# First products from transposed x with the norm's factor put on results, and another order in the scan, the prelude and the projections

## The chip, the cores and the metric

One core of a Trainium2 chip runs the whole layer in one launch. The metric is the device time of the run in microseconds; lower is better. Three runs of the kernel before were timed, and one more was profiled.

## The reference

x is 512 tokens by 2048 channels in float32. The layer is, cut to what matters:

```python
h = rmsnorm(x, norm_w)                  # x * rsqrt(mean(x*x) + eps) * w, per token
u = h @ w_in
z_ssm, xbc, dt_f, dt_b, q_a, kv_a, z_attn, g_ssm, g_attn = split(u)
xs, bm, cm = split(silu(dwconv(xbc, conv_w, conv_b)))        # conv over 4 tokens
y = ssd_scan(xs, dtf, a_f, bm, cm) + flip(ssd_scan(flip(xs), flip(dtb), a_b, flip(bm), flip(cm))) + d_skip * xs
y = rmsnorm_by_group(y * silu(z_ssm), ssm_norm_w)            # 4 groups of 512 channels
q  = rmsnorm(q_a, q_norm_w) @ w_uq                           # 16 heads, 128 + 64 (rotary)
kv = rmsnorm(kv_a[:512], kv_norm_w) @ w_ukv
o = softmax_attention(q, kv, rotary key) * silu(z_attn)
merged = sigmoid(g_ssm) * (y @ w_proj_ssm) + sigmoid(g_attn) * (o @ w_proj_attn)
out = rmsnorm(x + merged @ w_out, final_norm_w)
```

The factor rsqrt(mean(x*x) + eps) is one number per token. Since it is the same for all channels of a token, (x * w * factor) @ W equals ((x * w) @ W) * factor.

## The kernel before

**Products.** A float32 operand is split into a high part (ACT casts it to the reduced format, `wh`, L163 or L432) and a low part (DVE subtracts, `wl`, L164 or L433), and each product is three matmuls, high by high, high by low and low by high (`mm3`, L167 to L170; in the Strassen products L562 to L564). One matmul has a 128x128 stationary operand and 512 columns; a tile of 128 output channels takes 16 steps of three. Weights come in chunks of 128x1024 (512 KB) through three raw buffers (`wraw`) and three buffers for each part. `wchunk` (L157) issues load, cast and subtraction of a chunk with a priority offset `ahead[0]`, which is AHEAD (60) nearly everywhere.

**Order.** PE runs in the order in which the code issues its matmuls. The other engines' orders come from a scheduler that sorts by place in the program, moved ahead by the offset of `tc.high_priority`.

**Stages.** (1) x is loaded token by token rows, ACT squares it with a running sum (L210), a short DVE chain makes the factor, DVE scales x (L220), PE transposes it in 64 blocks (L225) and ACT and DVE split the result, times `norm_w`, into `h_h` and `h_l` (L229, L230). (2) Seven tiles: dt (`dtp`) and the six xbc tiles of scan group 0; after each, convolution and SiLU. Between them `h_sums` adds `h_h` and `h_l` back together and makes the sums of blocks of h that Strassen's scheme needs (S1, S2, S4). `dt_make` makes dt and writes it to the scratch `dt_d`. (3) Three gate projections (wz, wgs, wga), each as two column pairs of seven Strassen products (P1 to P7, `Strassen.pair`). A product is four chunks of 12 matmuls. Sums of weight blocks are made while they are loaded, by accumulating DMA (`w_more`), or by DVE. A headed pair takes P1 and P2 beforehand (`Strassen.head`, with P1b and P2b for the second pair); here only the ssm projection (`wps`) does that. (4) Four groups of the scan (`ssd_group`). Group 0 first transposes dt (`dt_turn`, L308) and sums it (`dt_sums`, L317 to L320). Every group loads B, C and four x tiles from scratch, transposes them (L872, `post_b`, `post_x`), makes local states ("loc", from `xw_h` and `xw_l`, L931 and L932) and adds up the diagonal parts ("yb", L1016). `y_norm` then gates and scales a y tile and `y_turn` transposes it (L848). Between these steps `gap()` runs fill work, the next group's xbc tiles and the qkv and za tiles, in shares listed in `shares`:

```python
shares = [0.7] * 2 + [0.8] * 6 + [1.25] * 10
left = [0, (10 * 48, 10 * 48, 9 * 48, 10 * 48)[g] / sum(shares)]
```

The first share stands ahead of the transpositions, the second ahead of "loc". After the last group the rest of za runs beside the normalising of the compressed q and kv (`compressed`, L1072 and L1074). (5) Sixteen attention heads, with their own fill; `r_sum` (L326) sums squares over channels for the q and kv norms with one matmul ("rp", L328) into the bank `pc`, which the diagonal sums use too. (6) The two branch projections and the output projection; the head of `wps` is fill of the last two attention heads, and what remains of it is issued by `fill.all()` after the loads and splits of S1 and S2 (operand sums read from scratch `yn_d`).

## Time and profile before

| | us |
|---|---|
| three timed runs | 2066.1, 2069.7, 2075.88 (median 2069.7) |
| the profiled execution, its own time | 2068.9 |
| its span | 2066.8 |
| PE busy in it | 1970.5 (95%) |
| DVE busy | 1463.1 (71%) |
| ACT busy | 959.3 (46%) |
| DMA, mean | 183 GB/s |

The span runs from the first to the last instruction of the profiled execution. Busy time is the union of an engine's instructions. PEld is the loading of stationary operands, which overlaps the matmuls. In a timeline a row has the start, the length, engine, line, operation and tiles, and in brackets how long the engine stood idle before it and what released it.

### The profile page before, as it was taken

To read this page: it belongs to the slowest core of one execution; us is meant where nothing else is said; L and a number is where in the kernel's file an instruction comes from. 1 tells how busy PE (TensorE), PEld (TensorE's weight loads), DVE (VectorE), ACT (ScalarE), POOL (GpSimd) and SP (SyncE) were. 2 spreads that over 40 slices of the span, in tenths; PEclk is the share of its full clock that TensorE was granted. 3 is DMA by queue.
4 is the path that set the end of the run, shared out by engine and by line. 5 is a ranking of instruction groups with operands and counts; after the bars stand their busy time and mean duration, and the time that the engine had idled before them with its cause. 6 is when DMAs were issued, how large, how long until landed. Compare 5 with 4: busy or idle time off the path is not lost.

```text
span 2066.8 us, 24703 instructions
## 1 busy us (share of the span) xinstructions
PE 1970.5 (95%) x9074; PEld 1627.3 (79%) x9074; DVE 1463.1 (71%) x1946; ACT 959.3 (46%) x1344; POOL 315.9 (15%) x337
## 2 busy tenths in 40 slices
PE   6999999999989999899899999999998999999998
PEld 5888888888867877787788788788877787888886
DVE  7976676676659689788786666667576888776342
ACT  6444444444444545445555344444444444443232
POOL 0011010010042151332420001110010111100110
PEclk9999999999999999999999999999999999999999
DMA  5567657656556837677564857873376876865332
GB/s 195 168 173 197 182 121 187 194 124 171 144 171 186 243 120 191 225 211 219 166 182 150 240 166 185 217 199 96 85 213 251 294 245 250 268 227 168 104 120 82
DMA packets 166584, 378.56 MB, mean 183 GB/s; under 512 B 16000, under 2 KB 65280, under 8 KB 165888
## 3 DMA queue, kind: packets, MB, share of 16 engines
q1 hardware_dynamic: 104688, 238.33, 35.2%
q0 software_dynamic: 26944, 92.29, 20.5%
q10 hardware_dynamic: 34832, 46.38, 6.3%
q8 instruction: 71, 1.16, 0.2%
q14 instruction: 49, 0.40, 0.1%
HBM read 325.03 MB, written 98.04 MB: 205 GB/s over the span
## 4 chain that ended last, share of the span: by engine, by line
PE 69%; DVE 11%; DMA 9%; issue 6%; ACT 2%; POOL 1%; SPq 0%; ACTq 0%; DVEq 0%; POOLq 0%
PE P L563 10%; PE P L564 10%; PE P L562 10%; PE f L1485 3%; PE f L1486 3%; PE f L1484 3%; PE za L168 2%; PE za L169 2%; PE za L170 2%; PE xbc L168 2%; PE xbc L169 2%; PE xbc L170 2%; DVE wl L164 2%; DVE sum L995 1%; DMA wraw<-wps 1%
## 5 line engine op out<-in xcount | busy, mean ns | idle before, releaser
L433 DVE TENSOR_TENSOR wl<-X,wh 128x1024 fp32r<-128x1024 f32 x152 | 185.2, 1222 | 81.8 <-ACT wh L432 81.3
L432 ACT CAST wh<-X 128x1024 fp32r<-128x1024 f32 x152 | 159.6, 1053 | 160.0 <-PE P L564 134.6
L164 DVE TENSOR_TENSOR wl<-wraw,wh 128x1024 fp32r<-128x1024 f32 (+2 forms) x148 | 175.4, 1186 | 81.7 <-ACT wh L163 76.4
L163 ACT CAST wh<-wraw 128x1024 fp32r<-128x1024 f32 (+2 forms) x150 | 145.3, 969 | 157.4 <-PE xbc L169 43.5
L433 DVE TENSOR_TENSOR wl<-wraw,wh 128x1024 fp32r<-128x1024 f32 x74 | 91.3, 1233 | 98.5 <-ACT wh L432 98.3
L168 PE MATMUL xbc<-h_h,wh 128*128 128x512 f32 x384 | 151.8, 395 | 0.0
L170 PE MATMUL xbc<-h_h,wl 128*128 128x512 f32 x384 | 150.2, 391 | 0.1
L169 PE MATMUL xbc<-h_l,wh 128*128 128x512 f32 x384 | 150.0, 391 | 0.0
L433 DVE TENSOR_TENSOR wl<-Y,wh 128x1024 fp32r<-128x1024 f32 x80 | 97.8, 1223 | 73.1 <-ACT wh L432 73.0
L563 PE MATMUL P<-wl,h_h 128*128 128x512 f32 x384 | 149.4, 389 | 0.0
L564 PE MATMUL P<-wh,h_l 128*128 128x512 f32 x384 | 149.4, 389 | 0.0
L562 PE MATMUL P<-wh,h_h 128*128 128x512 f32 x384 | 149.4, 389 | 0.0
L432 ACT CAST wh<-wraw 128x1024 fp32r<-128x1024 f32 x74 | 78.0, 1054 | 146.0 <-PE f L1486 71.0
L432 ACT CAST wh<-Y 128x1024 fp32r<-128x1024 f32 x80 | 84.2, 1053 | 114.8 <-PE P L564 95.3
L563 PE MATMUL P<-wl,S 128*128 128x512 f32 x288 | 112.4, 390 | 0.6 <-DVE wl L433 0.6
L564 PE MATMUL P<-wh,S 128*128 128x512 f32 x288 | 112.1, 389 | 0.0
L562 PE MATMUL P<-wh,S 128*128 128x512 f32 x288 | 112.1, 389 | 0.0
L170 PE MATMUL za<-h_h,wl 128*128 128x512 f32 x256 | 101.2, 395 | 5.0 <-DVE wl L164 5.0
L168 PE MATMUL za<-h_h,wh 128*128 128x512 f32 x256 | 102.3, 400 | 0.0
L169 PE MATMUL za<-h_l,wh 128*128 128x512 f32 x256 | 100.6, 393 | 0.0
L170 PEld LDWEIGHTS xbc<-h_h,wl 128*128 128x128 f32 x384 | 72.3, 188 | 16.1 <-DVE small L841 0.6
L168 PEld LDWEIGHTS xbc<-h_h,wh 128*128 128x128 f32 x384 | 72.6, 189 | 15.0 <-issue 0.2
(634 smaller groups left out, 5189.0 us busy)
## 6 DMA issues: line engine op xcount, KB each, us to landing
wraw<-wi SPq DMA_DIRECT2D x102, 512.0 KB, 4.1
da<-da_d SPq DMA_DIRECT2D x64, 256.0 KB, 4.4
T_wps<-wps POOLq DMA_DIRECT2D x32, 512.0 KB, 6.2
T_wpa<-wpa POOLq DMA_DIRECT2D x32, 512.0 KB, 9.9
wraw<-wo SPq DMA_DIRECT2D x32, 512.0 KB, 3.4
wraw<-wps SPq DMA_DIRECT2D x24, 512.0 KB, 5.0
xbc_d<-xbc ACTq DMA_DIRECT2D x24, 256.0 KB, 2.9
wraw<-wun SPq DMA_DIRECT2D x16, 384.0 KB, 3.1
```

The lines of the kernel that those rows point to most:

```text
L163: act.copy(h, raw)
L164: (dve if ahead[0] else pool).tensor_sub(l, raw, h.bitcast(F32))
L168: pe.matmul(out, wh, xh, start=start, stop=False)
L169: pe.matmul(out, wh, xl, start=False, stop=False)
L170: pe.matmul(out, wl, xh, start=False, stop=stop)
L432: act.copy(hi_, raw)
L433: dve.tensor_sub(lo_, raw, hi_.bitcast(F32))
L562: pe.matmul(bs[i], xh, wh, start=(j == 0), stop=False)
L563: pe.matmul(bs[i], xh, wl, start=False, stop=False)
L564: pe.matmul(bs[i], xl, wh, start=False, stop=(j == 7))
L1484: pe.matmul(acc, mh, wh, start=(start and k == 0), stop=False)
L1485: pe.matmul(acc, mh, wl, start=False, stop=False)
```

## The change

1. **Prelude.** x comes transposed from the host as well (`xt`, eight chunks of 128x1024). ACT squares each chunk, DVE multiplies by `norm_w`, and `x_split` splits into `h_h` and `h_l` without the token's factor. PE sums the squares by 64 one-column matmuls (`ss`), placed between the steps of the first three products (dt and two xbc tiles), which run interleaved. `factor` makes R, the factor of each token on all partitions. R is multiplied onto the three results; `x_t` is then multiplied by R and split again for all that follows. The next two xbc tiles run interleaved, the last two one after the other. `h_sums` adds blocks of `x_t` where it first had to rebuild them from the split parts. PE's own transpositions go.
2. **dt.** `dt_make` becomes a hook after P5 of the second pair of wz. Its result stays in SBUF; the scratch `dt_d` and its reload go, a small scratch `dv_d` comes.
3. **Gates.** wz runs headed: P1, P2 and P1b, then the first pair, P2b and the second pair. Its weights take 16 more chunk loads.
4. **Banks.** `r_sum` uses the bank `pa`.
5. **Scan.** The first two shares become 0.5 and 1.1; `y_norm` gets a priority offset of 30.
6. **za tail.** `ahead[0]` is 150 there.
7. **Attention.** 24 matmuls of fill ahead of the first head, not 15; the unit of fill is 2.77, not 2.8.
8. **ssm projection.** P2b becomes a fill entry of its own, and the loads and the split of S2 come after `fill.all()` with no priority.

On PE at the start of the program, before: `xt_239` to `xt_290` are the four token tiles of x, `dtp` the dt tile.

```order
L225 MATMUL mm<-cst,xt_239 128x128 x3
L225 MATMUL pa<-cst,xt_239 128x128 x2
L225 MATMUL pb<-cst,xt_239 128x128 x2
L225 MATMUL pc<-cst,xt_239 128x128
L225 MATMUL mm<-cst,xt_256 128x128 x3
...
L225 MATMUL pc<-cst,xt_290 128x128
L168 MATMUL dtp<-h_h,wh 128x512
L169 MATMUL dtp<-h_l,wh 128x512
L170 MATMUL dtp<-h_h,wl 128x512
```

All transpositions stand ahead of the first product. The same place on PE after the change, where `sq` is a chunk of squares, `cst` holds the ones and `rp` is the broadcast factor:

```order
L236 MATMUL ss<-cst,sq 128x1 x16
L168 MATMUL dtp<-h_h,wh 128x512
L169 MATMUL dtp<-h_l,wh 128x512
L170 MATMUL dtp<-h_h,wl 128x512
...
L236 MATMUL ss<-cst,sq 128x1 x8
L168 MATMUL xbc<-h_h,wh 128x512
L169 MATMUL xbc<-h_l,wh 128x512
L170 MATMUL xbc<-h_h,wl 128x512
...
L250 MATMUL rp<-dg,cst 128x128 x4
L168 MATMUL dtp<-h_h,wh 128x512
```

The transpositions are gone from ahead of the first product; 16 sums stand there, further sums between the products, and the four factor matmuls after the 17th step.

On DVE in the za tail (`raw`, `cq_l`, `ckv_l`: the normalising of the compressed q and kv; `ang`, `nn`: rotary angles), before, with eight instructions left out where the dots are:

```order
L164 TENSOR_TENSOR wl<-wraw,wh 128x1024 x3
L1085 CAST ang<-posi 128x512
L1086 TENSOR_SCALAR ang<-ang,cst 128x512
L1072 SCALAR_TENSOR_TENSOR raw<-raw,vec,R 128x512
L1087 TENSOR_SCALAR nn<-ang 128x512
L1072 SCALAR_TENSOR_TENSOR raw<-raw,vec,R 128x512 x2
...
L1072 SCALAR_TENSOR_TENSOR raw<-raw,vec,R 128x512
L1074 TENSOR_TENSOR cq_l<-raw,cq_h 128x512
L1072 SCALAR_TENSOR_TENSOR raw<-raw,vec,R 128x512
L1074 TENSOR_TENSOR ckv_l<-raw,ckv_h 128x512
L164 TENSOR_TENSOR wl<-wraw,wh 128x1024
```

Eighteen instructions stand between the third weight split and the fourth. The same place on DVE after the change:

```order
L164 TENSOR_TENSOR wl<-wraw,wh 128x1024 x3
L1113 CAST ang<-posi 128x512
L1114 TENSOR_SCALAR ang<-ang,cst 128x512
L1100 SCALAR_TENSOR_TENSOR raw<-raw,vec,R 128x512
L1115 TENSOR_SCALAR nn<-ang 128x512
L1100 SCALAR_TENSOR_TENSOR raw<-raw,vec,R 128x512 x2
L164 TENSOR_TENSOR wl<-wraw,wh 128x1024
L1102 TENSOR_TENSOR cq_l<-raw,cq_h 128x512 x3
```

The fourth weight split moved from behind eighteen instructions to behind six.

On ACT ahead of the ssm projection, before: `S__13064` is S1, `S__13073` S2, `kk<-P1b` the unloading of P1b, and the three casts after S2 are weights of P2b:

```order
L432 CAST S__13064<-xraw 128x1024
L432 CAST wh<-wraw 128x1024
L525 COPY kk<-P1b 128x512 x2
L432 CAST S__13064<-xraw 128x1024
L435 ACTIVATE S__13073<-xraw 128x1024 x2
L432 CAST wh<-wraw 128x1024 x3
L432 CAST wh<-X 128x1024 x2
```

S2 stands ahead of the three weights. The same place on ACT after the change (`S__13110` is S1, `S__13312` S2):

```order
L421 CAST S__13110<-xraw 128x1024
L421 CAST wh<-wraw 128x1024
L514 COPY kk<-P1b 128x512 x2
L421 CAST S__13110<-xraw 128x1024
L421 CAST wh<-wraw 128x1024 x3
L424 ACTIVATE S__13312<-xraw 128x1024
L421 CAST wh<-X 128x1024
L424 ACTIVATE S__13312<-xraw 128x1024
L421 CAST wh<-X 128x1024 x3
```

The casts of P2b's weights moved ahead of S2, whose two halves stand among the first casts of X.

The diff, cut to what the steps below speak of:

```diff
-    xs_t = []
-    for t in range(TT):
-        xt = xp.tile([P, D], F32, name=f"xt{t}")
-        ss = few(2)
-        for i in range(2):
-            cs = slice(i * D // 2, (i + 1) * D // 2)
-            nc.sync.dma_start(xt[:, cs], a["x"][t * P:(t + 1) * P, cs])
-            scr = xp.tile([P, D // 2], F32, tag="scr", bufs=1, name="scr")
-            act.activation(scr, xt[:, cs], AF.Square, accum_out=ss[:, i:i + 1])
-        v = few(1)
-        dve.tensor_add(v, ss[:, 0:1], ss[:, 1:2])
-        dve.tensor_scalar(v, v, 1.0 / D, EPS, ALU.mult, ALU.add)
-        r = small_rsqrt(v, 1, lambda n: few(1))
-        for i in range(2):
-            cs = slice(i * D // 2, (i + 1) * D // 2)
-            if t >= TT - 2 and i == 1:
-                act.activation(xt[:, cs], xt[:, cs], AF.Copy, scale=r)
-            else:
-                dve.tensor_scalar_mul(xt[:, cs], xt[:, cs], r)
...
-    def x_out(k):
-        nw = vec[:, V_NORM + k:V_NORM + k + 1]
-        act.activation(h_h[:, k, :], tps[k % 8], AF.Copy, scale=nw)
-        dve.scalar_tensor_tensor(h_l[:, k, :], tps[k % 8], nw, h_h[:, k, :].bitcast(F32), ALU.mult, ALU.subtract)
...
+    def x_split(k):
+        act.copy(h_h[:, k, :], x_t[:, k, :])
+        dve.tensor_sub(h_l[:, k, :], x_t[:, k, :], h_h[:, k, :].bitcast(F32))
+
+    squares, early = [], []
+    ahead[0] = 1
+    for j in range(8):
+        xs = x_t[:, 2 * j:2 * j + 2, :].rearrange("p k t -> p (k t)")
+        nc.sync.dma_start(xs, a["xt"][j])
+        if j in (0, 1, 3):
+            early.append(wchunk(a["wi"][(T_DT, T_XBC + 4, T_XBC + 5)[len(early)], 0], 1024))
+        squares.append(sxq("sq"))
+        act.activation(squares[j], xs, AF.Square)
+        for k in (2 * j, 2 * j + 1):
+            dve.tensor_scalar_mul(x_t[:, k, :], x_t[:, k, :], vec[:, V_NORM + k:V_NORM + k + 1])
+            x_split(k)
...
+    def square_sums(j):
+
+        for k in range(2):
+            for t in range(TT):
+                pe.matmul(ss[t][:, 0:1], squares[j][:, k * SEQ + t * P:k * SEQ + (t + 1) * P], ones[:, 0:1],
+                          start=(j + k == 0), stop=(j == 7 and k == 1))
...
+        rp = pc("rp")
+        for t in range(TT):
+            pe.matmul(rp[:, t * P:(t + 1) * P], ones, dg[:, t * P:(t + 1) * P], start=True, stop=True)
+        act.copy(R, rp)
...
-        rp = pc("rp")
+        rp = pa("rp")
...
-            yield from self.second(1, b, lambda i: sum_tile("p5"), None, "P2b")
+
+        def head_end(self):
+            return self.second(1, self.p1[1], lambda i: sum_tile("p5"), None, "P2b")
...
+    def xbc_done(i, p_):
+        v_ = sx.tile([P, SEQ], F32, tag="v", bufs=1, name="xbc_v")
+        dve.tensor_mul(v_, p_, R)
+        o = st("xbc")
+        put(xbc_d[0][i], conv_silu(v_, (4 + 12, 4 + 16)[i - 4], o, lambda n: o))
...
+    firsts = [mm(n) for n in ("dtp", "xbc", "xbc")]
+    order = "AABABABC" + "ABC" * 3 + "A" + "BCBC" + "ACAC" + "BABAC" + "ABC" * 3 + "A" + "BCBCBCC"
...
+    square_sums(0)
+    square_sums(1)
+    for i in together([gemm_steps(p_, win(t), h_h, h_l, w_) for p_, t, w_ in zip(firsts, (T_DT, T_XBC + 4, T_XBC + 5), early)], order):
+        if i % 2 == 1 and i // 2 < 6:
+            square_sums(2 + i // 2)
+        if i == 16:
+            factor()
...
+    dve.tensor_mul(v_, firsts[0], R)
...
+    for k in range(KT):
+        dve.tensor_mul(x_t[:, k, :], x_t[:, k, :], R)
+        x_split(k)
+        if k in (1, 3):
+            xbc_done(4 + k // 2, firsts[1 + k // 2])
+    for i in together([xbc_gen(0, i, None) for i in (0, 1)], "AAA" + "AB" * 13 + "BBB"):
+        pass
+    for i in (2, 3):
+        h_sums(i - 2)
+        run(xbc_gen(0, i, None))
...
-    gates[0].hooks = {(0, "P5"): [lambda: h_ops.load("S3"), lambda: [h_part("S3", 256, q) for q in range(2)]]}
+    gates[0].hooks = {(0, "P5"): [lambda: h_ops.load("S3"), lambda: [h_part("S3", 256, q) for q in range(2)]],
+                      (1, "P5"): [dt_make]}
     gates[2].hooks = {(1, "P7"): [h_back, lambda: [h_part("x21", 256, q) for q in range(2)]]}
-    gates[0].first_columns(0)
-    run(xbc_gen(0, 3, None))
-    for p_ in gates:
+    run(gates[0].head())
+    run(gates[0].pair(0, True))
+    run(gates[0].head_end())
+    run(gates[0].pair(1, True))
+    for p_ in gates[1:]:
...
-    dt64 = tmp2("dt64")
-    with tc.high_priority(offset=LOAD_AHEAD):
-        nc.sync.dma_start(dt64, dt_d)
...
-        shares = [0.7] * 2 + [0.8] * 6 + [1.25] * 10
+        shares = [0.5, 1.1] + [0.8] * 6 + [1.25] * 10
...
-                y_norm(c, g, y)
+                with tc.high_priority(offset=30):
+                    y_norm(c, g, y)
...
+    ahead[0] = 150
...
-    fill.run(15)
+    fill.run(24)
...
-        unit = 2.8 if hd < AH - 2 else 2
+        unit = 2.77 if hd < AH - 2 else 2
...
+            fill.add("head", part_of_head(wps))
...
-    for w in ("S1", "S2"):
-        with tc.high_priority(offset=LOAD_AHEAD):
+    for w, ahead_ in (("S1", LOAD_AHEAD), ("S2", 0)):
+        if w == "S2":
+            fill.all()
+        with tc.high_priority(offset=ahead_):
             y_ops.raws[w] = [cols.tile([P, 1024], F32, tag="Y", bufs=4, name="xraw") for q in range(2)]
             for q in range(2):
                 nc.sync.dma_start(y_ops.raws[w][q], yn_d[w][:, q * 1024:(q + 1) * 1024])
         if w == "S1":
             wps.first_columns(0)
         C(y_ops, w)()
-    fill.all()
```

## Rows read from the trace of the kernel before

**Rows 1.** Cores view, then the page's busy line of PE.

```profile
core 0: 2066.8 us, clock 0.984
PE 1970.5 (95%) x9074; PEld 1627.3 (79%) x9074; DVE 1463.1 (71%) x1946; ACT 959.3 (46%) x1344; POOL 315.9 (15%) x337
```

**Rows 2.** Waits of PE: line, releaser, us in total, times, longest.

```profile
PE mm L225 <- DVE xt L220: 19.3, 4, 11.1
PE turn L848 <- ACT y L842: 10.0, 4, 3.8
PE loc L169 <- DVE xw_l L932: 8.0, 5, 2.4
...
PE P2b L562 <- ACT wh L432: 6.3, 1, 6.3
PE pb L308 <- DMA dt<-dt_d: 5.4, 1, 5.4
...
PE za L170 <- DVE wl L164: 5.0, 1, 5.0
PE pb L872 <- ACT xT L883: 4.7, 8, 0.7
PE rp L328 <- DVE y L1019: 4.1, 2, 2.6
PE s L1242 <- ACT kh L1197: 3.7, 3, 1.2
```

**Rows 3.** Timeline (start, us, engine, line, what) of ACT and PE, 0 to 110.

```profile
5.87 1.06 ACT L210 ACTIVATE scr<-xt 128x1024 f32<-128x1024 f32 x1 [2.71 <-DMA xt<-x]
...
7.50 1.06 ACT L210 ACTIVATE scr<-xt 128x1024 f32<-128x1024 f32 x1 [0.48 <-DMA xt<-x]
...
11.07 0.90 PE L225 MATMUL mm<-cst,xt 128*128 128x128 f32 x3 [11.07 <-DVE xt L220]
11.77 0.64 PE L225 MATMUL pa<-cst,xt 128*128 128x128 f32 x2
...
32.47 0.50 PE L168 MATMUL dtp<-h_h,wh 128*128 128x512 f32 x1
...
108.77 0.39 PE L562 MATMUL P<-wh,h_h 128*128 128x512 f32 x1
```

**Rows 4.** Instructions by line, 0 to 110: busy us, mean ns.

```profile
L163 ACT CAST wh<-wraw 128x1024 fp32r<-128x1024 f32 x14 | 14.8, 1055 | 25.1 <-PE xbc L169 18.6 <-PE dtp L169 4.4 <-issue 2.1
...
L164 DVE TENSOR_TENSOR wl<-wraw,wh 128x1024 fp32r<-128x1024 f32 x12 | 14.6, 1214 | 0.3 <-ACT wh L163 0.3
```

**Rows 5.** Timeline of PE at the first diagonal products of the scan.

```profile
642.93 1.00 PE L1016 MATMUL yb<-xT,G 128*128 128x64 f32 x8
643.77 0.44 PE L979 MATMUL cb<-CT,BT 128*128 128x128 f32 x2
```

**Rows 6.** DMA issues 108 to 300 (KB, median landing), chain of waits at 112.

```profile
wraw<-wz SPq DMA_DIRECT2D x6, 512.0 KB, 3.4
...
112.24 11.73 DMA X<-wz
```

**Rows 7.** Entry of scan group 0: SP and PE timelines, DMA issues.

```profile
572.12 3.81 SPq L894 DMA_DIRECT2D xs<-xbc_d  x4
...
585.25 0.47 PE L168 MATMUL xbc<-h_h,wh 128*128 128x512 f32 x1
...
xs<-xbc_d SPq DMA_DIRECT2D x4, 256.0 KB, 5.8
```

**Rows 8.** Timeline of DVE in the scan of group 0, a weight split.

```profile
667.35 2.06 DVE L164 TENSOR_TENSOR wl<-wraw,wh 128x1024 fp32r<-128x1024 f32 x1
```

**Rows 9.** Busy time (count) by engine, 600 to 700; granted clock, DMA share.

```profile
600.00:700.00 100.00, 95.55 (x440) 79.12 (x439) 91.65 (x127) 51.98 (x74) 31.00 (x26) 0.97 0.69 194
```

**Rows 10.** Timeline of DVE in the za tail.

```profile
1165.37 1.22 DVE L164 TENSOR_TENSOR wl<-wraw,wh 128x1024 fp32r<-128x1024 f32 x1
```

**Rows 11.** Timeline of ACT ahead of P2b of the ssm projection.

```profile
1583.73 2.26 ACT L435 ACTIVATE S__13073<-xraw 128x1024 fp32r<-128x1024 f32 x2 [0.20 <-DMA xraw<-yn_S]
```

146 lines of the change are left out of this document (73 added, 73 removed).

## The prediction

> **What bounds the kernel now.** I read the cores view first, then the page's busy line, then the waits of PE, then the timelines at those waits. The span is 2066.8 us and PE is busy for 1970.5 of it [rows 1], so PE's queue is the bound and about 96 us of the span are PE standing still. The waits of PE name nearly all of them [rows 2]: 19.3 us at the four transposition groups at the start, 10.0 at the transpositions of finished y rows ("turn"), 8.0 at the scan's local states ("loc"), 6.3 at P2b of the ssm projection, 5.4 at the first dt transposition, 5.0 in the za tail, 4.7 at the x transpositions of the scan, 4.1 at the two norm sums ("rp") and 3.7 at attention scores. The matmul count hardly changes: 64 transpositions go, 64 one-column sums and four 128-column products come. So the change can pay only by taking away waits, and each is priced where it stands.
>
> The profiled run took 2068.9 us, 2.1 more than its span; the median of the three timed runs is 2069.7. I make the sum on the span and add 2.1 at the end.
>
> **Part 1, the start.** Before, PE's first instruction stands at 11.07, the first product at 32.47 and the first gate product at 108.77 [rows 3]. Between the last two lie 7 tiles of 48 matmuls: 76.3 us, 0.227 a matmul. The change must do the same 76.3 us, started earlier, and adds the sums.
> Start: the first 512 KB half of x has landed at 5.87, the next at 7.50, 1.63 apart [rows 3]. The first weight chunk now comes second, so ACT's first cast waits to about 7.5; a cast of 128x1024 takes 1.055 [rows 4], a square 1.06 [rows 3], two half-size casts of h 1.3 by estimate (a little over half of 1.055 each), so the squares of chunk 0 are there at about 9.6 and those of chunk 1 at 12.3.
> Sums: 64 fp32 matmuls are 128 records (fp32 matmuls stand as two records each in the rows). The trace has none with one column. The nearest is L1016 with 64 columns: eight records from 642.93 to 643.77, 0.105 each [rows 5]. At the very start records go slower: three transpositions in 11.07 to 11.77, 0.23 each [rows 3]. I take 0.21 for the 32 records ahead of the first product (6.7 us, from 9.6, done at about 16.4) and 0.105 for the other 96 (10.1 us). The four products of the factor are eight records, with the slow start of the first products some 2.5 us more. 16.4 + 10.1 + 76.3 + 2.5 = 105.3, against 108.77: **−3**. The ends: if a record cost by its columns alone, at 0.227 for 512, 128 one-column records would be nearly free; PE would then wait for ACT, whose last squares come near 26 (7.5 + three casts, eight squares and eleven half casts of 0.65), with 36 of the 48 first steps of three matmuls still to do: 26 + 24.6 + 43.6 + 2.5 = 96.7, −12. If all 128 went at 0.21 it would be 10 more than the forecast, +7. I take the 64-column row because it has the same 128x128 weights.
> The Trainium skill, "TensorE: Matmul & The Clock Gate", section "Wait — 56ns, not 53.3ns?", says that the start-to-start time of matmuls follows the columns down to a floor of about 25 ns; by it the 128 records would take some 3 us, an estimate from that page, and the start would gain over 10. The 64-column row speaks against it here, as its eight records took 0.105 each; the rule stays as a rival.
> Cover: ACT has three casts, eight squares and sixteen casts of h (about 22 us from 7.5, done near 29), ahead of PE's need at every step. After the factor DVE multiplies x by it (16 x 0.6) and splits again (16 x 0.6), with weights at 1.214 a chunk [rows 4] and the convolutions between: about 34 us of DVE work from 39 to the second pair of xbc tiles, which starts near 62. It fits by a few us, and if it does not, the second pair of tiles waits (rival 3). The loads of the start are the same eight halves of x and the weight chunks, in another order. In PE's order the sums stand two chunks ahead and then between every second product step, so none of them has to wait for squares.
>
> **Part 2, the gate wz by the headed way.** It needs 16 more 512 KB loads, and its second operand halves go through the three raw buffers. Six such loads on SP's queue landed in 3.4 us (median), but an X chunk at 112 took 11.73 [rows 6]. A chunk lasts PE 12 matmuls, 2.7 us, so three buffers cover 8.2. No load has yet stood there in both halves, so I lean to the 3.4 and take **+1** (−0.5 to +15; the upper end is four landings like the 11.73, 3.5 over each).
>
> **Part 3, entry of the first scan group.** dt64 now stays in SBUF, so the 5.4 us [rows 2] go. What is late next: the four xs loads, issued by 572.1 to 575.9, landing 5.8 after issue [rows 7]. They move up by the removed issue, half a us, and end near 581; PE came to fill work at 585.25 [rows 7]. Then 582 to 583 instead, and 0.5 to 1 less fill ahead of it: **−3** (−8 to −1).
>
> **Part 4, shares.** The two first gaps get 12.7 and 27.9 fill matmuls in place of 18.0 and 18.0, since the group's 480 are divided by 18.9 and no longer 18.7 shares. The second gap stands ahead of "loc": 9.9 x 0.227 = 2.2 us more cover, against waits of at most 2.4 [rows 2]. **−7** of 8.0 (−8 to 0). The price is 1.2 us less cover ahead of the transpositions, whose longest wait is 0.7 [rows 2]: **+2** (0 to +5).
>
> **Part 5, y_norm at a higher priority.** The four turns wait 10.0 us [rows 2]. In group 0 a DVE weight split of 2.06 us stands inside the chain that makes y [rows 8]; in the new order the split stands ahead of the chain or behind it, and other short steps lie between. Half of the 10.0 is taken: **−5** (−10 to 0). DVE pays: it is busy for 91.65 of 100 us there [rows 9], and whatever passes in front delays sums and weight splits. I give back **+4** (0 to +12).
>
> **Part 6, r_sum in another bank.** "rp" waits for the y sum to free its bank, 4.1 [rows 2]; pa has no such reader: **−4** (−4.1 to 0).
>
> **Part 7, za tail.** The fourth weight split stands on DVE behind eighteen steps of normalising and angles and starts at 1165.37 [rows 10]; PE waits 5.0 [rows 2]. With the priority of 150 it stands behind six, so twelve steps and the waits for their loads are out of its way: **−5** (−5 to 0).
>
> **Part 8, attention.** Three heads stop 1.2 us each at the scores [rows 2], since no fill is left there. 24 matmuls of early fill and 2.77 in place of 2.8 move the gaps so that two of the heads still have none: **−1** (−4 to 0).
>
> **Part 9, ssm projection.** P2b waits 6.3 [rows 2]: ACT does S2 first, 2.26 us [rows 11], and S2's loads and the X loads stand before P2b's weights. Now three casts for P2b stand ahead of S2: **−4** (−6.5 to −1), as the first S1 cast waits for its own load still.
>
> The other parts (the dt chain at a hook of the gates, the operand sums from x, the unloading of dt) go beside 76 and 150 us of products with DVE idle in part: 0.
>
> **Sum:** −3 + 1 − 3 − 7 + 2 − 5 + 4 − 4 − 5 − 1 − 4 = −25. Span 2066.8 − 25 = 2041.8, and with the 2.1 the time is **2044** (25.7 under the median, 24.9 under the profiled run's own).
>
> **Rivals.**
> 1. *The one-column sums are cheap.* For it: the operation reads one column. Against it: the 64-column row. The start is −12 in place of −3, so 2035; chance 0.20. The Trainium skill's page named in part 1 has this as its rule.
> 2. *The scan's gain is lost on DVE.* For it: 91.65 of 100 us busy in group 0. y's chain, the state splits and weight splits are all on that queue, so what no longer waits at loc and turn waits at "G", xbc or za. Parts 4 and 5 then give nothing (their −6 in the sum goes) and 3 more are lost: 2053. Against it: in the other groups DVE is idle for a fifth of the time. Chance 0.17.
> 3. *The factor on results does not pay at the start.* The re-split of h is late for the second pair of tiles, or all sums go at 0.21: the start is +7 in place of −3: 2054; chance 0.08. Against it: DVE's work fits by a few us, and records at 0.21 are seen only at the start.
> 4. *Slower: the headed gate starves.* The 16 added raw halves land as the 11.73 one did; each then stops PE for 11.7 − 8.2 = 3.5 us. It passes the gains of the rest (25 + 1) from 8 such loads on; with all 16, 56 − 26 = +30 against the profiled run: 2099. For it: two halves of every operand now come at the same time. Against it: six loads of that kind land in 3.4. Chance 0.05.
> The forecast itself has 0.50.
>
> **Range and chances.** From the cheap sums with a good scan (2035 less 9: −5 more at the turns, −4 not given back) to the lost scan with part of a bad start (2053 plus 7): **2026 to 2060**. A difference of 0.5%, 10.3 us, is about what a measurement of this kernel can tell from none. Faster means under 2059.4: the forecast, rivals 1 and 2 and 3 nearly whole: 0.86; same 0.09; slower 0.05.
>
> **What would show it.** The first one-column row: at 0.105 a record the forecast, well under that rival 1. The first gate product at 105 (97 for rival 1, 115 for rival 3). No wait at the first dt transposition but up to 2 at the xs transpositions. Waits of loc under 1, turns about 5, rp and za none, P2b about 2. DVE's busy share over 92 in group 0 with new waits at G or xbc would be rival 2; PE waits on DMA through the raw buffers between 110 and 260, rival 4. Wrong altogether would be PE's busy time moving by over 15 us.

## The result and the profile after

The changed kernel takes 2077.6 us in the median of 20 runs (2066.8 to 2087.6), the kernel before 2070.4 in the median of 20 runs of the same series (2062.4 to 2075.9). The ratio is 1.0035, with an interval of 1.0022 to 1.0049: some 7 us slower, where 26 us faster were forecast, and outside the range. The profiled execution of the changed kernel took 2082.8, 5 us more than its median, so single stages are read below against several executions.

The cores view of the changed kernel and the page's busy line of PE, which answer to [rows 1]:

```profile
core 0: 2081.0 us, clock 0.981
PE 1990.0 (96%) x9146; PEld 1646.4 (79%) x9146; DVE 1471.7 (71%) x1970; ACT 973.3 (47%) x1355; POOL 312.4 (15%) x335
```

PE's busy time rose by 19.5 us, past the 15 that the prediction had named as the sign of being wrong altogether. Some 15 of them stand ahead of the first gate product.

The waits of PE of the changed kernel (tile and line waited at, releaser, us in total, times, longest), which answer to [rows 2]:

```profile
PE turn L874 <- ACT y L868: 13.0, 4, 7.8
PE P L552 <- DVE wl L422: 10.1, 10, 3.9
PE ss L236 <- ACT sq L226: 8.9, 1, 8.9
PE P L551 <- ACT wh L421: 6.6, 4, 2.7
PE P2b L551 <- ACT wh L421: 3.9, 1, 3.9
PE vp L1208 <- DVE wl L164: 3.8, 1, 3.8
PE pb L898 <- DMA xs<-xbc_d: 3.5, 1, 3.5
PE qkv L170 <- DVE wl L164: 3.5, 3, 1.6
PE pb L898 <- DMA BT<-xbc_d: 3.3, 1, 3.3
PE pb L898 <- DVE b_l L904: 3.2, 1, 3.2
PE pb L898 <- ACT dec L310: 3.1, 1, 3.1
```

The waits that were to go are gone: no dt, no rp, no za row, and loc is down from 8.0 to 0.8. Others stand in their place: the transpositions of the scan (L898) wait on six different releasers, "turn" waits more than before, and the products of wz wait for their split weights: 8.0 us between the first gate product and the first fill product, where the kernel before waits 0.6.

The stages by the first row of each kind on PE, in us. "Start" ends at the first gate product, "gates" at the first fill product behind them, "entry" at the first loc; then come the scan to the loc of group 3, the rest up to the first t product (the q projection), t to the first scores, the scores to the ssm projection, the projections, and the output up to PE's last row. The second row is another execution of the kernel before, and the rows below are the experiments of the next section.

| kernel | start | gates | entry | scan | to t | t to s | to P1b | proj. | output |
|---|---|---|---|---|---|---|---|---|---|
| before | 108.8 | 458.4 | 22.3 | 417.2 | 184.2 | 32.2 | 344.2 | 314.0 | 176.3 |
| before2 | 108.8 | 458.1 | 24.0 | 420.7 | 182.5 | 34.0 | 345.2 | 310.0 | 175.7 |
| changed | 113.7 | 469.8 | 25.1 | 419.8 | 173.2 | 40.5 | 343.2 | 310.7 | 175.5 |
| start_alone | 114.3 | 464.6 | 23.5 | 422.0 | 184.1 | 29.8 | 343.2 | 310.8 | 176.2 |
| nohead | 109.0 | 464.1 | 26.0 | 417.3 | 173.3 | 40.3 | 340.3 | 310.3 | 176.3 |
| dense | 101.5 | 468.5 | 25.0 | 416.3 | 174.9 | 39.7 | 342.2 | 307.3 | 175.8 |
| dense_nohead | 107.4 | 462.5 | 24.7 | 417.0 | 175.1 | 40.4 | 337.1 | 311.3 | 176.3 |
| za_old | 113.8 | 470.1 | 25.2 | 416.5 | 181.0 | 36.1 | 342.9 | 310.2 | 176.1 |
| rest | 108.8 | 458.7 | 25.6 | 416.4 | 173.5 | 41.3 | 341.4 | 311.7 | 176.0 |
| best1 | 108.9 | 457.9 | 24.0 | 416.0 | 181.0 | 37.1 | 338.9 | 311.1 | 176.3 |

Start and gates lose 16 us in the profiled execution; the scan gains nothing; most of what is won ahead of t is lost behind it.

The timeline of PE at the start of the changed kernel (start, us, engine, line, operation, count):

```profile
8.91 6.98 PE L236 MATMUL ss<-cst,sq 128*128 128x1 f32 x32 [8.91 <-ACT sq L226]
...
15.75 0.78 PE L168 MATMUL dtp<-h_h,wh 128*128 128x512 f32 x1
...
18.46 3.41 PE L236 MATMUL ss<-cst,sq 128*128 128x1 f32 x16
...
36.38 2.00 PE L236 MATMUL ss<-cst,sq 128*128 128x1 f32 x16
38.24 0.48 PE L168 MATMUL dtp<-h_h,wh 128*128 128x512 f32 x1
...
39.71 1.84 PE L236 MATMUL ss<-cst,sq 128*128 128x1 f32 x16
...
113.70 0.39 PE L551 MATMUL P<-wh,h_h 128*128 128x512 f32 x1
```

From one start to the next, sixteen records of sums go at 0.204 each up to 36, and at 0.107 behind it; the products between go at 0.452 on the mean and then at 0.23 to 0.25. So PE runs at its lower level (1.2 GHz) until 36.4 and at the upper one (2.4) from there.

### The profile page after: what moved, and what is told of

Its sections match the earlier page's. It is cut to its first block, busy times and chain, and to the rows that moved or that the text cites. A ratio compares the mean times of both kernels' runs of the same rounds, so it can differ in the third digit from the quotient of the medians.

```text
span 2081.0 us, 24930 instructions
## 1 busy us (share of the span) xinstructions
PE 1990.0 (96%) x9146; PEld 1646.4 (79%) x9146; DVE 1471.7 (71%) x1970; ACT 973.3 (47%) x1355; POOL 312.4 (15%) x335
## 3 DMA queue, kind: packets, MB, share of 16 engines
q1 hardware_dynamic: 106928, 246.59, 35.9%
## 4 chain that ended last, share of the span: by engine, by line
PE 73%; DVE 12%; DMA 8%; issue 3%; ACT 2%; SPq 0%; POOL 0%; ACTq 0%; DVEq 0%; POOLq 0%
PE P L552 10%; PE P L553 10%; PE P L551 10%; PE f L1518 3%; PE f L1517 3%; PE f L1519 3%; PE xbc L168 3%; PE xbc L169 3%; PE xbc L170 3%; DVE sum L1021 2%; PE za L168 2%; PE za L169 2%; PE za L170 2%; DVE wl L164 2%; DVE wl L422 1%
## 5 line engine op out<-in xcount | busy, mean ns | idle before, releaser
L422 DVE TENSOR_TENSOR wl<-X,wh 128x1024 fp32r<-128x1024 f32 x144 | 175.4, 1222 | 70.6 <-ACT wh L421 70.4
L421 ACT CAST wh<-X 128x1024 fp32r<-128x1024 f32 x144 | 151.2, 1053 | 147.7 <-PE P L553 123.9
L422 DVE TENSOR_TENSOR wl<-wraw,wh 128x1024 fp32r<-128x1024 f32 x82 | 101.1, 1234 | 119.1 <-ACT wh L421 119.0
L421 ACT CAST wh<-wraw 128x1024 fp32r<-128x1024 f32 x82 | 86.3, 1053 | 161.3 <-PE f L1519 71.6
L551 PE MATMUL P<-wh,h_h 128*128 128x512 f32 x352 | 137.0, 389 | 0.0
L552 PE MATMUL P<-wl,h_h 128*128 128x512 f32 x352 | 137.0, 389 | 0.0
L553 PE MATMUL P<-wh,h_l 128*128 128x512 f32 x352 | 137.0, 389 | 0.0
L552 PE MATMUL P<-wl,S 128*128 128x512 f32 x288 | 113.8, 395 | 5.8 <-DVE wl L422 5.8
L1021 DVE TENSOR_TENSOR_SCAN sum<-da,scn 128x512 f32<-128x512 f32 x64 | 88.0, 1389 | 0.0
```

The source lines that it names most:

```text
L421: act.copy(hi_, raw)
L422: dve.tensor_sub(lo_, raw, hi_.bitcast(F32))
L551: pe.matmul(bs[i], xh, wh, start=(j == 0), stop=False)
L552: pe.matmul(bs[i], xh, wl, start=False, stop=False)
L553: pe.matmul(bs[i], xl, wh, start=False, stop=(j == 7))
L1021: dve.tensor_tensor_scan(sums[dd], flat(da), mask, 0.0, ALU.add, ALU.mult)
```

## The experiments

Ratios are to the kernel before, run beside each on the same chip. The changed kernel's is 1.0035.

**warm**: four matmuls of constants on PE while it has nothing to do.

```diff
+    wm = mm("warm")
+    for _ in range(4):
+        pe.matmul(wm, ident, cst[:, 0:SEQ], start=True, stop=True)
     ss = [pa("ss"), pa("ss"), pb("ss"), pb("ss")]
```

> The changed kernel with four 512-column float32 matmuls of constants ahead of the first one-column sum (their result is not used); nothing else differs. Theory A (the start loses because PE's clock is still at its lower level when the sums begin, and they do not raise it): the dummies run while PE had nothing to do, the sums then go at 0.107 a record from the first on, the first gate product comes at about 102 in place of 113.7, and the time falls by about 10. Rival B (one-column sums bring the clock down again, or cost 0.21 whatever went before): the sums of the first five chunks stay at 0.21, the first gate product stays within 3 us of 113.7, the time within 3.

Measured: 1.0016 (1.0000 to 1.0032). Stretches of this run (us, PE, PEld, DVE, ACT, POOL busy with counts, granted clock of PE, DMA share, GB/s):

```profile
10.00:15.00 5.00, 5.00 (x29) 3.61 (x27) 4.49 (x7) 5.00 (x8) 0.00 (x0) 0.98 1.02 419
15.00:20.00 5.00, 5.00 (x19) 4.42 (x19) 5.00 (x10) 4.63 (x7) 0.00 (x0) 0.50 0.98 401
...
25.00:30.00 5.00, 5.00 (x21) 4.63 (x20) 1.92 (x4) 1.63 (x3) 0.00 (x0) 0.50 0.01 3
...
```

Neither theory as written, though the first gate product at 112.0 is what rival B said. The dummies bring PE to the upper level, the first sums go fast, and then, with the sums running, the granted clock falls from 0.98 to 0.50, with PE busy throughout. It stays there till near 32. So the level that the dummies had brought was lost while PE ran one-column sums without a pause.

**dense**: the same sums by 512-column matmuls, ones stationary.

```diff
-            for t in range(TT):
-                pe.matmul(ss[t][:, 0:1], squares[j][:, k * SEQ + t * P:k * SEQ + (t + 1) * P], ones[:, 0:1],
-                          start=(j + k == 0), stop=(j == 7 and k == 1))
+            pe.matmul(ss, ones, squares[j][:, k * SEQ:(k + 1) * SEQ], start=(j + k == 0), stop=(j == 7 and k == 1))
```

> The changed kernel with the squares summed by 16 float32 matmuls of 512 columns (the ones stationary, the squares moving) in place of 64 of one column; the sum then stands on all partitions, and the four matmuls of the factor go. Theory A2 (the one-column sums are what lets PE stay at its lower level until 18 to 36): PE reaches the upper level within 8 us of its first sum, as it did after the dummies, and stays there; the sums cost 16 x 1 us; the first gate product comes at 102 to 106 in every execution, the time falls by 7 to 11 against the changed kernel. Rival N (the level at the start is a matter of the execution, whatever runs): the first products are still at 0.45 past 18.

Measured: 0.9996 (0.9983 to 1.0009), by the ratios 8 us below the changed kernel. PE's timeline:

```profile
8.11 6.02 PE L235 MATMUL ss<-sq,cst 128*128 128x512 f32 x8 [8.11 <-ACT sq L226]
13.56 0.79 PE L168 MATMUL dtp<-h_h,wh 128*128 128x512 f32 x1
14.19 0.39 PE L169 MATMUL dtp<-h_l,wh 128*128 128x512 f32 x1
...
101.51 0.39 PE L541 MATMUL P<-wh,h_h 128*128 128x512 f32 x1
```

PE is at the upper level from the second product on and stays there: the granted clock reads 1.00 in every stretch to 100. The four other traces with these sums (combo, dense_nohead, split_a, s3_pool) have their first product at the upper pace at 13.9 to 14.5. A chunk's sums with its two product steps take 3.1 us (18.4 to 21.6), as those of one column take at the upper level in the changed kernel (39.71 to 42.88: 3.2). The cost of the sums is the same. Of the 12.2 us of the start, 10 are the clock level: 48 records at 0.204 in place of 0.107 and 24 products at 0.452 in place of 0.227. Theory A2 holds.

The level with one-column sums is a matter of the execution too. In **scan_old**, whose start is that of the changed kernel word for word:

```profile
18.23 1.90 PE L236 MATMUL ss<-cst,sq 128*128 128x1 f32 x16
...
104.93 0.39 PE L551 MATMUL P<-wh,h_h 128*128 128x512 f32 x1
```

Here the rise comes at 18, and the first gate product stands at 104.9. In six executions with this start the rise came at 18.2 (scan_old), 24.5 (nohead), 30.5 (nohead_early), 36.1 (start_alone), 36.2 (za_old) and 36.4 (the changed kernel). That is where the wider spread of the changed kernel's runs can come from; it was not tested run by run.

**sums_pool**: squares added up on GpSimd, four sums left.

```diff
+            half = squares[j][:, k * SEQ:(k + 1) * SEQ]
+            pool.tensor_add(acc, acc, half)
...
+        if i == 24:
+            square_sums()
```

> The changed kernel with the squares added up on GpSimd (15 adds of 128x512), so that 4 one-column sums are left of 64, behind the 25th product step; R comes 13 steps later. Theory A (sums and low clock are what the start lost): products begin near 11, PE is at the full clock by 16, the first gate product comes at 95 to 99 in place of 113.7, the time falls by 14 to 18. Rival C (the start is bound by the supply of split h or by the second split, not by the sums): PE waits for h or for x times R take the place of the sums, and the first gate product comes later than 106.

Measured: 1.0070 (1.0044 to 1.0097). Rival C: PE begins its products at 10.85, waits for weights (4.7 us at 42.2, 2.9 at 85.2) and not for h, is at the lower level again behind the first of these waits (granted clock 0.50 from 42 to 50), and has its first gate product at 116.2.

**start_alone**: the new start and the dt change alone.

```diff
-    run(gates[0].head())
-    run(gates[0].pair(0, True))
-    run(gates[0].head_end())
-    run(gates[0].pair(1, True))
+    gates[0].first_columns(0)
+    run(xbc_gen(0, 3, None))
...
-        shares = [0.5, 1.1] + [0.8] * 6 + [1.25] * 10
+        shares = [0.7] * 2 + [0.8] * 6 + [1.25] * 10
...
-    ahead[0] = 150
...
```

> The changed kernel with everything undone but the new start and the dt change (wz as before, old shares, priorities, bank, fill and S2 order). Theory L (the start wins nothing at the clock level it meets, and holds x so long that the first gate weights come late): first gate product between 104 and 113 by execution, 4 to 6 us of waits between it and 140, the time 2 to 9 us above the kernel before. Rival M (the start gains its 3 us): 2 to 4 us below.

Measured: 1.0045 (1.0029 to 1.0060). Theory L: first gate product at 114.3, 5.3 us of waits from there to 141. The start and the dt change alone lose as much as the whole change, as far as the intervals can tell.

**rest**: the kernel before with the edits of scan, banks, za, attention and ssm projection, and none of the start, the head of the gates or dt.

```diff
-        rp = pc("rp")
+        rp = pa("rp")
...
-        shares = [0.7] * 2 + [0.8] * 6 + [1.25] * 10
+        shares = [0.5, 1.1] + [0.8] * 6 + [1.25] * 10
...
-                y_norm(c, g, y)
+                with tc.high_priority(offset=30):
+                    y_norm(c, g, y)
...
+    ahead[0] = 150
...
-    fill.run(15)
+    fill.run(24)
...
```

> The kernel before with the shares, the y_norm priority, the bank of r_sum, the za priority, the attention fill and the S2 order of the changed kernel, without the new start, the headed wz and the dt change. Theory J (start and headed gate are what made the whole no faster): this one is faster than the kernel before by 5 to 12 us. Rival K (these edits only move waits): within 3 us of the kernel before.

Measured: 0.9973 (0.9958 to 0.9988), 2062.4 us. Theory J, at its lower end. **This version beats both kernels.** Its gain is 4 to 6 us over all stages. Only "to t" (−10) and "t to s" (+8) differ by more than some 4 us from the kernel before, whose own two executions differ by up to 4 us in a stage. Which of its edits the gain comes from is not shown.

**before2**: the kernel before, once more.

> The kernel before once more, for a second trace of it: how much its stages differ from one execution to the next with nothing changed. If the clock at the start is a matter of the single execution also here, the first gate product moves by more than 1 us from 108.8; if the old start is steady, it stays at 108 to 109.5. Scan stages are expected within 3 us of the first trace.

First gate product at 108.8 again: the old start is steady, its first product stood behind transpositions that all ran before. Entry, scan and projections differ by 2 to 4 us between the two.

**nohead**: wz without the head (the first hunk of start_alone).

> The changed kernel with the gate wz run as before, P1 and P2 inside each pair, its first X columns loaded ahead of the last xbc tile; dt stays at its hook. Theory D (the headed way of wz starves on its loads between 110 and 225): the stretch from first gate product to the first fill product falls from 469.8 to about 459 and the waits of P1b and P on their split weights there from 8 to under 1; the time falls by 8 to 11. Rival E (the loads of x and weights at the start are late for any first gate product): waits of 4 us or more remain at the first gate products, and the time falls by less than 5.

Measured: 1.0020 (1.0004 to 1.0037). Between the theories: the waits that starved P1b go, but 5.0 us of waits come between the first gate product and 135, as rival E said, and the gates take 464.1 and not 459. Two waits in the head of the changed kernel, from PE's timeline:

```profile
142.85 0.50 PE L551 MATMUL P1b<-wh,h_h 128*128 128x512 f32 x1 [1.07 <-ACT wh L421]
...
154.82 0.50 PE L552 MATMUL P<-wl,S 128*128 128x512 f32 x1 [1.61 <-DVE wl L422]
```

The stretch from 140 to 150 of the changed kernel, and behind it that of the kernel before (columns as in warm):

```profile
140.00:150.00 10.00, 8.00 (x33) 5.74 (x31) 4.84 (x5) 5.15 (x6) 0.85 (x1) 1.00 1.04 375
```

```profile
140.00:150.00 10.00, 10.00 (x46) 8.29 (x45) 7.46 (x10) 4.22 (x4) 0.00 (x0) 1.00 0.54 172
```

The DMA engines are full in the head (share 1.04 against 0.54), and PE waits for weights: 4.2 us between 138 and 155.

The longest wait of the changed kernel's gates stands elsewhere, at the second pair's P5. DVE there, PE's wait, and the stretch behind it (columns as in warm):

```profile
216.76 0.42 DVE L273 TENSOR_SCALAR p<-e 64x512 f32<-64x512 f32 x1 [1.99 <-DMA zs_d<-p]
217.21 3.34 DVE L274 RECIPROCAL p<-p 64x512 f32<-64x512 f32 x1
220.48 2.28 DVE L422 TENSOR_TENSOR wl<-X,wh 128x1024 fp32r<-128x1024 f32 x2
```

```profile
221.69 0.79 PE L552 MATMUL P<-wl,S 128*128 128x512 f32 x1 [3.85 <-DVE wl L422]
```

```profile
221.70:228.00 6.30, 6.30 (x15) 4.95 (x16) 6.30 (x7) 1.21 (x2) 0.00 (x0) 0.51 0.01 3
```

L273 and L274 are `dt_make` at its hook. Its step waits for a gate tile to be written out, then takes a reciprocal of 3.34 us, and the weight splits that PE needs stand behind both. Behind the wait PE is at the lower level again: 13 matmuls take 0.43 each, 2.6 us more. In five of the six traces with the head a wait of 2.3 to 4.0 us stands at this place (0.2 in sums_pool); in the seven without the head, where `dt_make` comes later, none is over 0.2. No run has the head with `dt_make` elsewhere, so the two edits share this cost.

**dense_nohead**: both edits.

> The changed kernel with the squares summed by 16 matmuls of 512 columns and with wz run without the head. If start and head add up as they did apart (first gate product 101.5 in place of 113.7; gates 464 in place of 469.8), the profiled span comes near 2063 + 2.1 less what the later stages vary: 2056 to 2062 in the median, below both kernels. If the head only hides loads that come late anyway, the gates stay above 467 and the time at 2064 or more.

Measured: 0.9985 (0.9975 to 0.9996). They do not add up: start and gates together take 569.9, with the head 570.0. The faster PE arrives, the longer it waits for the first X columns (5.8 us at 107.4). Before, the two took 567.2.

**nohead_early**, **combo**: the block sums on GpSimd and earlier.

```diff
-        dve.tensor_sub(view4(s1), x(1, 0), x(1, 1))
+        pool.tensor_sub(view4(s1), x(1, 0), x(1, 1))
```

> The changed kernel without the headed wz, and with the sums of blocks of x (S1 to S4) taken from DVE to GpSimd and issued ahead of the third xbc tile. Theory O (wz's first X columns load late because their buffers lie where the block sums are, and these end at 103 in a full DVE queue): the X loads are issued 6 us or more earlier against the first gate product than the 5.4 us of the run without the head, the waits of about 5 us at the first gate products fall under 2, the gates' stretch falls from 464 to 460. Rival P (the loads are late because of the DMA queues): X issues earlier but the waits stay above 4.

> The changed kernel with the sums by 512-column matmuls, without the headed wz, the block sums on GpSimd and early, and the za priority of before. If theories A2 and O hold, the start ends at 102 to 106, the gates take 459 to 461, and the rest is as in the run of the other edits alone: 2055 to 2060, below both kernels. If either falls, 2062 or more.

Measured: 1.0077 (1.0049 to 1.0105) and 1.0067 (1.0041 to 1.0093). Both lose: a step of 128x1024 took 2.4 to 8.5 us on GpSimd, and PE waited 7.3 us at 91.5 for a weight split of DVE. X left at 107.8 and 102.3, no earlier than in nohead (103.6) and dense_nohead (100.8), and PE, late itself, waited not at the first gate product but some way behind it (5.4 and 9.2 us near 134). Theory O was not told from P by these.

**split_a**: x in two tiles, the first X columns over the half that is done first (two tiles of 16 KB a partition).

> The kernel dense_nohead with x kept in two tiles of 32 KB per 4 partitions' worth (one for each half of the block sums) and the first X columns laid over the half that is done first. Theory O (X's loads wait for the last block sum, because their buffers lie over those of the sums): the X loads leave 3 us or more earlier against the first gate product, the waits at the first gate products fall from 4 to 5 us to under 2, the gates' stretch from 464 to 460 or 461, the time by 2 to 4. Rival P (the loads are late because of the queue and the DMA engines): X leaves earlier or not, the waits stay above 4.

Measured: 0.9988 (0.9978 to 0.9998), no different from dense_nohead. X leaves at 99.8 and not 100.8, and the wait is 5.9 (5.8 there). The place of the buffers is not the cause.

**s3_pool**: the S3 reload on another queue.

```diff
-        nc.sync.dma_start(t, src[:, q * 1024:(q + 1) * 1024])
+        (pool if src is h_d["S3"] else nc.sync).dma_start(t, src[:, q * 1024:(q + 1) * 1024])
```

> The kernel split_a with the two S3 reloads on GpSimd's queue in place of SP's, where they stood ahead of wz's first weight and X loads and left at 81 and 96.6. Theory Q (the first X columns are late because they stand in SP's queue behind the S3 reload, which waits for the last block sum of DVE): X leaves 4 us or more earlier than 99.8, the 5.8 us at the first gate product fall under 2, the time falls by 3 to 5 against split_a, to 2060 to 2062. Rival R (what they stand behind are wz's first two weight chunks, whose raw buffers wait for DVE's splits of the xbc weights): X leaves at most 2 us earlier and the wait stays above 4.

Measured: 0.9989 (0.9977 to 1.0002). Rival R in its signs: X no earlier, and a wait above 4. SP's queue in this run, then a split on DVE, then the first gate product on PE:

```profile
89.93 10.43 SPq L449 DMA_DIRECT2D wraw<-wz  x2
100.41 2.25 SPq L449 DMA_DIRECT2D X<-wz  x4
```

```profile
98.74 1.22 DVE L419 TENSOR_TENSOR h_l<-xraw,h_h 128x1024 fp32r<-128x1024 f32 x1
```

```profile
108.65 0.80 PE L548 MATMUL P<-wh,h_h 128*128 128x512 f32 x1 [6.68 <-ACT wh L418]
```

X stands in SP's queue behind wz's second weight chunk. That chunk's raw buffer holds the S3 reload until DVE has split it, at 98.74 to 99.96, and X leaves 0.45 later. So it is a split of S3 that holds the buffer here, and not one of the xbc weights that rival R named.

**before_busy**: the kernel before with 20 us of idle DVE work.

```diff
+                for _ in range(32):
+                    dve.tensor_add(idle, idle, h_h[:, 0, :].bitcast(F32))
             h_sums(i // 2)
```

> The kernel before with 33 idle DVE steps of 128x512 (0.6 us each, about 20 us) issued ahead of its second block sums; their result is not used. Theory S (DVE's backlog between 45 and 110 is what makes the first gate products wait in the changed kernel): the last block sum ends 8 us or more later than at 82.8, X leaves later than 100 in place of 95.3, and PE waits 4 us or more in all at xbc and the first gate products; the time rises by 3 to 8. Rival T (DVE has the room): waits under 2, time within 2.

Measured: 1.0106 (1.0084 to 1.0129). SP's queue in this run, and the first gate product on PE:

```profile
96.13 24.17 SPq L463 DMA_DIRECT2D wraw<-wz  x3
120.35 2.60 SPq L463 DMA_DIRECT2D X<-wz  x4
```

```profile
127.69 0.79 PE L562 MATMUL P<-wh,h_h 128*128 128x512 f32 x1 [18.77 <-ACT wh L432]
```

Theory S, and more than it said: 20 us more on DVE become 18.8 us of PE standing still, by the same chain. In the kernel before the chunk and X leave at 94.9 and 95.3. The stretch from 60 to 110 of the changed kernel (columns as in warm, DVE the third):

```profile
60.00:110.00 50.00, 50.00 (x222) 41.30 (x221) 49.82 (x62) 31.12 (x40) 0.00 (x0) 1.00 0.44 148
```

And of the kernel before:

```profile
60.00:110.00 50.00, 50.00 (x222) 41.39 (x221) 45.46 (x54) 25.88 (x31) 1.92 (x2) 1.00 0.59 192
```

**scan_old**: old shares, no y_norm priority, in the changed kernel. **rest_noscan**: the same in rest.

```diff
-        shares = [0.5, 1.1] + [0.8] * 6 + [1.25] * 10
+        shares = [0.7] * 2 + [0.8] * 6 + [1.25] * 10
...
-                with tc.high_priority(offset=30):
-                    y_norm(c, g, y)
+                y_norm(c, g, y)
```

> The changed kernel with the old shares (0.7, 0.7) and no priority for y_norm. Theory F (the two scan edits win about as much as they lose, since PE's waits at loc come back at the transpositions and the turn waits move): loc waits of 6 to 8 us return, waits at the x transpositions fall from 16 to 9 or so, the time stays within 3 us. Rival G (the scan edits gain as predicted, 6 us or more): the time rises by 6 or more.

> The run of the other edits alone (rest) with the old shares and no priority for y_norm. Theory F (the two scan edits win about as much as they lose): 2061 to 2064, as that run's 2062.4. Rival G (they gain as predicted, 6 us net or more): 2068 or more, no faster than the kernel before.

Measured: 1.0049 (1.0032 to 1.0066) and 0.9986 (0.9975 to 0.9996), 2077.2 and 2064.9 us. Neither is told from its partner (1.0035 and 0.9973). In each pair the partners lie 3 us apart by the ratios. If the two scan edits gain, it is 0 to 6 us by both pairs together, not the 10 of terms 4 and 5 ahead of what was given back. The waits between 560 and 1130, summed over all rows, say the same: 34.4 and 35.9 us in the two traces of before, 36.8 in the changed kernel, 37.0 in scan_old, 33.7 in rest, 34.9 in rest_noscan (31.4 in best1, the lowest of all). Mostly their names change. The two edits were always taken back together, so neither is judged alone.

**za_old**, **best1**: the za priority of 60, in the changed kernel and in rest.

```diff
-    ahead[0] = 150
```

> The changed kernel with the chunk priority of 60 in the za tail, as before. Theory H (the 5 us won in the za tail come back at the first products behind it, t and vp, because the rotary steps and their loads then come later): the stretch from the last scan group to t grows by 4 to 6 us, the stretch from t to the first scores shrinks by as much, and the time stays within 2 us. Rival I (the za edit gains its 5 us): the time rises by 4 to 6.

> The kernel before with the shares, the y_norm priority, the bank of r_sum, the attention fill and the S2 order, without the za priority (the run of the other edits alone, less that one). Theory H (the za priority only moves its 5 us): within 2 us of that run, 2061 to 2065. Rival I (it gains): 2066 to 2070.

Measured: 1.0044 (1.0022 to 1.0066) and 0.9980 (0.9962 to 0.9997). Theory H in the time, which is the same within the intervals, and half of it in the stages: with the old priority "to t" is 8 us longer in both pairs and "t to s" only 4 shorter, so 3.4 us of the stages are left as a gain that the times can't tell from none. In the changed kernel the price stands here, on PE and then on DVE:

```profile
1216.08 0.58 PE L1208 MATMUL vp<-wl,ckv_h 128*128 128x256 f32 x1 [3.80 <-DVE wl L164]
```

```profile
1214.81 1.22 DVE L164 TENSOR_TENSOR wl<-wraw,wh 128x1024 fp32r<-128x1024 f32 x1
```

The weight split that vp waits for stands on DVE behind four rotary steps. These begin at 1212.4, in za_old at 1211.5; but PE comes to t at 1201.6, in za_old at 1206.6, so it is PE that is early.

## Why the prediction was wrong

**Part 1, the size of the sums.** The step that failed is "0.105 for the other 96". A record did take 0.107, as the 64-column row [rows 5] said, and the 32 ahead of the first product took 6.84 as forecast (6.7). But 48 more went at 0.204, so all sums took 21.9 and not 16.8, and 24 product matmuls took 0.452 each, 5.4 us over their 0.227, where 2.5 was allowed for slow products and factor together. Rival 3 named this ("all sums go at 0.21", 2054) and was set aside with "records at 0.21 are seen only at the start". That reading was wrong: the trace of the kernel before has transpositions at 0.23 each 14 us behind PE's first row, and again in the scan, both behind a wait (columns as in rows 3):

```profile
25.17 0.90 PE L225 MATMUL mm<-cst,xt 128*128 128x128 f32 x3 [6.30 <-DVE xt L220]
...
672.37 1.12 PE L848 MATMUL turn<-cst,y 128*128 128x128 f32 x4 [3.75 <-ACT y L842]
```

I took the slow rate to be a matter of when, and in these runs it went with what PE did: with the one-column sums the level stayed low until 18 to 36 or fell, with the same sums in 512 columns it was up by 14.5 in all five traces. Where the level rose early, in scan_old, the first gate product came at 104.9 against the forecast 105.3, so the sum was right for the upper level. Rival 1 fell: a float32 sum with a full 128x128 stationary block took 0.107 a record at the upper level too. The Trainium skill's page "TensorE: Matmul & The Clock Gate" (section "Wait — 56ns, not 53.3ns?") gives a floor of about 25 ns between starts; these sums stay at four times that, and the measurement decides.

**Part 1, the cover.** "It fits by a few us" was right for what it looked at: PE has no wait from the first product to 139 in the changed kernel. It looked no further than the next tiles of PE. Behind the second split stood the block sums, their way out and back, a raw buffer, a weight chunk and X; before, the last block sum was split by 83, in the changed kernel by 111 (by 101 to 109 in nohead, start_alone, scan_old, dense and dense_nohead). These block sums are the prediction's "operand sums from x", which it put at 0. The cost came 50 us later, as 5 to 7 us at the first gate products (nohead, start_alone, dense_nohead). Whether the waits that stand in P1b and the first P5 with the head have the same cause is not shown.

**Part 2, the head.** Forecast +1, with +15 as the end; the gates took 11.4 more. Of it 4.2 are waits between 138 and 155, where the DMA engines were full, as rival 4 had it. Another 6.5 are `dt_make`: the wait of 3.85 at 221.7 and 2.6 of matmuls at the lower level behind it. The step that failed is the line "The other parts (the dt chain at a hook of the gates, the operand sums from x, the unloading of dt) go beside 76 and 150 us of products with DVE idle in part: 0." It looked at how busy DVE is and not at what stands behind the chain in its queue. Nor was the term independent of part 1: with dense sums start and gates take 570 us with and without the head. In the time the head with this hook costs 2 to 3 us by the ratios (1.0035 against 1.0020, 0.9996 against 0.9985), whose intervals overlap.

**Parts 3 to 6, the scan.** Each named wait went as said (dt 5.4 to 0, loc 8.0 to 0.8, rp 4.1 to 0), "turn" did not (10.0 to 13.0), and the sum of −13 came to nothing, since the total of waits stayed at 34 to 37 us. The step that failed is what was given back, +4 in part 5 and +2 in part 4: 17 us of waits went (dt, loc, rp) and 19 came, 11.7 at the transpositions, 4.5 at qkv and 3 at "turn". The three longest turns did come down, from 3.8, 3.5 and 2.3 to 1.9, 1.9 and 1.4. But one behind them, without a wait before, waits 7.8; the traces with both scan edits all have such a wait (7.1 to 7.8), those without them have none. On DVE in the changed kernel:

```profile
973.06 0.69 DVE L864 TENSOR_TENSOR y<-y,z 128x512 f32<-128x512 f32 x1 [1.13 <-DMA z<-zs_d]
```

The gate z of that y is loaded from 968.8 on, when y itself is done (965.9 to 966.6); before, its load left at 946.5 and y came at 956.7. At the entry, too, it can be followed, in PE's timeline of the changed kernel and then in ACT's:

```profile
593.15 1.08 PE L898 MATMUL pb<-cst,BT 128*128 128x128 f32 x4 [3.29 <-DMA BT<-xbc_d]
597.29 1.11 PE L898 MATMUL pb<-cst,xs 128*128 128x128 f32 x4 [3.05 <-ACT dec L310]
```

```profile
594.44 0.62 ACT L921 CAST c_h<-CT 128x512 fp32r<-128x512 f32 x1 [6.22 <-DMA CT<-xbc_d]
595.07 1.28 ACT L307 ACT_TABLE_LOAD   x1
...
596.86 0.38 ACT L310 ACTIVATE dec<-pb 128x256 f32<-128x256 f32 x1
```

Without dt's load PE comes early and waits for BT instead. ACT has the cast of CT at the head of its queue, and the exponentials that free the bank "pb" stand behind it and a table load. I had named xs as what is late next; it was BT, and then CT on an engine I had not looked at.

**Part 7.** The 5.0 in the za tail went, and t and vp wait 5.5, where they waited 2.1 in za_old and 1.9 and 3.6 in the traces of before. So about 3.4 of the 5 came back. "So twelve steps are out of its way" asked when PE comes to the next product and not whether DVE, behind its rotary steps, has that product's weights ready.

**Parts 8 and 9.** Near: the scores' waits (their two rows together) fell from 5.5 to 4.7, P2b from 6.7 to 4.7 (−2, forecast −4).

**The rivals.** They were priced as if only one could come, and several came in part. By stages the profiled execution lies 39 us over the forecast: start 8, gates 10, entry and scan 18 (13 against the second trace of before), the rest 3. The range was built from single rivals and so ended at 2060. That the prices of rival 3 (+10), rival 2 (+9), part 2's upper half (+10) and part 7 coming back (+5) add up to 34, and so to the median, is partly luck: the largest piece of the gates was none of these, and part 7 came back by 3.4.

## What to carry to other kernels

Before you price a wait that goes, ask what the engine's next input is and when it lands; where the waits of a stage add up to the same sum whatever you take away, look for something behind them all that sets the pace (here it was not found). Work put on an engine that is full (here DVE, 45.5 of 50 us) is paid where its queue next holds a buffer back, which can be far from the edit; a chain that looks free by DVE's busy share, like `dt_make`, costs what it holds up. And start a pipeline's first engine early only with work under which its clock was seen to rise, and only if the inputs of the stage behind are early too: rest, which leaves the start alone, has the lowest ratio here (0.9973), though its interval overlaps those of best1, rest_noscan, dense_nohead and split_a.

## What the runs showed of the hardware

Unexpected were three things. One-column matmuls keep PE busy by every row of the profile (5.00 of 5.00 us) and still ran with the granted clock going from 0.98 to 0.50; with the same sums in 512 columns it stayed up. The moment of the rise under one-column sums moved between 18 and 36 us from execution to execution of the same code, and in the changed kernel the clock column reads 1.00 in that stretch, where the pace of the records (0.204 against 0.107) says otherwise (two stretches of the changed kernel, columns as in warm). And two float32 sums of 512 columns cost PE the same 1.8 to 1.9 us a chunk as eight of one column at the upper level.

```profile
25.00:30.00 5.00, 5.00 (x20) 4.52 (x20) 1.72 (x4) 1.06 (x1) 0.00 (x0) 1.00 0.02 3
...
35.00:40.00 5.00, 5.00 (x30) 4.35 (x29) 3.88 (x7) 2.54 (x5) 0.00 (x0) 1.00 0.01 2
```

The first holds 20 records and the second 30, at the same reading of 1.00; so I went by the pace.
